# A two-layer f32r transformer trunk: inverse roots per token in the MLP, and its up tiles dealt ten and six to the two groups of down steps

## The chip, the cores and the metric

One core of one Trainium2 chip. The metric is the device time of one execution in microseconds (us); where several runs were made, their median. Engines: PE multiplies, DVE (VectorE), ACT (ScalarE) and POOL (GpSimd) work on elements, SP issues the loads.

## The reference

The trunk has two layers on 256 tokens of width D = 2048. Each adds an attention part, which the change leaves alone, and then an MLP with FF = 8192 hidden features:

```python
def rms_norm(x, g):
    y = x * rsqrt(mean(x * x, axis=-1, keepdims=True) + EPS)
    return y * g

def sq_relu_mlp(h, g, w_in, w_out):          # w_in 2048 x 8192, w_out 8192 x 2048
    return square(relu(rms_norm(h, g) @ w_in)) @ w_out

for layer in range(2):
    ...
    h = h + sq_relu_mlp(h, norm_mlp[layer], w_mlp_in[layer], w_mlp_out[layer])
```

## The kernel before

**Number format.** All products are of fp32 values. Each factor is split into two parts of the type fp32r, hi (a cast) and lo (what the cast left), and the kernel adds hi·hi, hi·lo and lo·hi. The tokens stay on chip in this form (mlpx and hid: hi in one half, lo in the other). The weights come from memory as "raw" tiles of 128x1024, 512 KB each, issued on SP into six buffers. ACT casts hi (L197; L251 and L273 for the down weights), DVE subtracts lo (L200, L252, L274). Three tiles are prepared ahead of the matmuls that use them; hi has four buffers, lo five.

**Order.** PE runs in the order in which the program is written. On DVE, ACT, POOL and SP a scheduler of the framework orders the instructions at build time, by a simulated time of its own. The calls later(…, n) and start_side(…) put small pieces of work behind a given number of the main steps' slots.

**The MLP.** The hidden features come in four chunks of sixteen tiles of 128. An up tile U multiplies two raw tiles: 16 matmuls of 512 columns with hi (they give hi·hi and the product of the tokens' lo in one go) and 16 of 256 columns with lo, all into one PSUM bank. Then ACT copies the bank's upper half (L475, low), DVE adds the lower (L1186, up), DVE takes relu and multiplies by the inverse root of the norm (L1168), ACT squares, and the square is split for the down matmuls (L1126, L1127). Because the inverse root is applied here, an up tile needs it only when it is finished, not when it is multiplied.

The output of a chunk is added up in two groups (n = 0 and 1) of 1024 columns each, but for the last chunk, whose second half is done by features or by tokens in another way. In a group, the first five pairs of hidden tiles go through a step S of Strassen's kind (seven, seven products for eight): four prepared weight pieces, 21 matmuls of 512 columns; DVE forms differences of the raw weights in place (L246 to L250), and of each pair of hidden tiles the block sums s23 and s14 (L1149 to L1152). The other three pairs go through two direct steps each, A and B, one for each 512 of the columns: 12 matmuls with one raw tile. At a group's end its banks are added to sums on chip (L1094; copies L1092 in the first chunk). In the last chunk merged (L1039) adds six sums of products to these, and turned (L1023) transposes them back and adds them to h.

**PSUM.** Of the eight banks, four ("acc") serve the up tiles and the group's sums 11, 21 and 12; two serve p1, p5 and 22; one each p6 and p7. Of the four, a group holds three from its first S on. p1, p5 and 22 share two, so that B and A steps stand where 22 has a bank.

**Turns.** A chunk's first group runs with the last eight up tiles of the same chunk, the second with the first eight of the next one. weave writes out the order. The first chunk's eight up tiles ahead of any down step are H (two tiles in halves) and T (pairs, each with two banks). In the program of before this gives, for each chunk:

```
H T2 T4 T6                                              (once)
U8 S0 U9 S1 U10 S2 U11 S3 U12 S4 U13 A5 U14 A6 U15 B5 B6 A7 B7      first group
U0 S0 A5 U1 S1 A6 U2 S2 A7 U3 S3 U4 S4 U5 U6 B5 U7 B6 B7            second group, U of the next chunk
```

A finished pair of up tiles, 2j and 2j+1, is what S_j, or A_j and B_j, of the chunk multiplies.

**The inverse root.** inverse_root sums the squares of h over the features by one fp32 matmul with a matrix of -1, whose result stands alike in all 128 partitions; DVE scales it (L576), and POOL raises 128x256 values to the power of -0.5 (L577).

Of the kernel before, what the change touches and what calls it, by code (L numbers as in the profile page):

```python
# [16 lines left out]
P = 128  # L17
D = 2048
T = 256
# [23 lines left out]
WARM_UP = 10  # L43


SEVEN = [5, 5]
BY_TURNS = 8


def weave(sevens, late):  # L50

    first, second = [], []
    u = BY_TURNS if late else 0
    for j in range(sevens):
        first += [("U", u), ("S", j)]
        u += 1
    direct = list(range(sevens, KT // 2))
    last = u + BY_TURNS - sevens
    if late:
        a, b = list(direct), list(direct)  # L60
        for i, f in enumerate(range(u, last)):
            second.append(("U", f))
            while a and 2 * a[0] + 1 < f:
                second.append(("A", a.pop(0)))
        second += [("B", j) for j in b[:-1]] + [("A", j) for j in a] + [("B", b[-1])]
    else:
        steps, first = first, []
        a = list(direct)
        for step in steps:
            first.append(step)  # L70
            if step[0] == "S" and a:
                first.append(("A", a.pop(0)))
        b = [("A", j) for j in a] + [("B", j) for j in direct]
        for f in range(u, last):
            second += [("U", f)] + ([b.pop(0)] if f > u else [])
        second += b
    return first + second


def mlp_steps(l):  # L80

    steps = [("H", 0, None)] + [("T", 0, f) for f in range(FIRST_UP, BY_TURNS, 2)]
    steps = [(c, 0) + (kind, f) for kind, c, f in steps]
    for c in range(NCH):
        for n in range(2 if c < NCH - 1 else 1):
            for kind, i in weave(SEVEN[l], n == 0):
                steps.append((c + 1 if kind == "U" and n == 1 else c, n, kind, i))
    return steps

# [40 lines left out]
def trunk(  # L130
# [161 lines left out]
    def start_side(g):  # L292
        active.append(g)
# [19 lines left out]
    def mm(o, lhs, rhs, start, stop):  # L313
        nc.tensor.matmul(o, lhs, rhs, start=start, stop=stop)
# [255 lines left out]

    def inverse_root(acc, name):

        ps = ps_y.tile([P, 512], F32, name="inv", tag="y")
        mm(ps[:, :T], neg_ones[:], acc[:], True, True)
        ri = const.tile([P, T], F32, name=f"ri_{name}", tag="ri")
        nc.vector.tensor_scalar(ri[:], ps[:, :T], -1.0 / D, EPS, op0=ALU.mult, op1=ALU.add)  # L576
        nc.gpsimd.tensor_tensor(  # L577
            ri[:], ri[:], neg_half[:, 0:1].to_broadcast([P, T]), op=ALU.pow
        )
        return ri  # L580

    def normed_heads(banks, eps_ms, gain, dst, wait=2):

# [245 lines left out]
    def mlp_stream(l):  # L829
        def unit(c, g, j):  # L830
            ap = w_down[l, 4 * g : 4 * g + 4, 2 * c + j // 4]
            ap = ap[:, :, 256 * (j % 4) : 256 * (j % 4) + 256]
            return ap.rearrange("o p x -> p o x")

        for c, n, kind, i in mlp_steps(l):
# [41 lines left out]
    def delayed(g, n):  # L877
        for _ in range(n):
            yield
        yield from g  # L880
# [57 lines left out]
    later(scale_gains, 10)  # L938

    mstat = {}  # L940
    xg = None
    xs = None

# [50 lines left out]
            two_tiles(y, [lambda b, i=i: evac(i, b) for i in (o, o + 1)], WO_ORDER)  # L994

    def mlp(l, xg_, sq, h, done):
        inv = {}
        later(lambda: inv.update(ri=inverse_root(sq, f"mlp{l}")), 4)
        sums = [heads4(f"d{l}_{i}") for i in range(4)]

        def summed(m, g):
# [45 lines left out]
                count[0] += 1  # L1047

        hid = new_act(f"hid{l}")
        sevens = SEVEN[l]  # L1050

        class Group:

# [75 lines left out]
        def block_sums(c, j, a, b):  # L1129
# [7 lines left out]
            if not whole:  # L1137
                x = nar.tile([P, T], F32R, name="s_x", tag="bias", bufs=6)
                last = (x[:, :P], x[:, P:], s14[:, P:])
            elif j != 3:  # L1140
                x = wide.tile([P, 512], F32R, name="s_x", tag="wide")
                last = (x[:, :T], x[:, T:], s14[:])
            else:
                x = [nar.tile([P, T], F32R, name="s_x", tag="bias", bufs=6) for _ in range(2)]
                last = (x[0][:], x[1][:], s14[:])
# [19 lines left out]
        def finish(c, f):  # L1165
            squares, factors = chunks[c]
            a = squares[f]
            nc.vector.scalar_tensor_tensor(  # L1168
                out=a[:], in0=a[:], scalar=0.0, in1=inv["ri"][:], op0=ALU.max, op1=ALU.mult
            )  # L1170
# [20 lines left out]

        staged = [] if l == 1 else None

        def add_second(c):
            yield from merged(1)

        def merge_first(staged=staged):
            if l == 1:
                yield from turned(3, None)
# [7 lines left out]
            yield from turned(1, done)  # L1207

        groups = {}
        for c, n, kind, i in mlp_steps(l):  # L1210
            if kind == "H":
                halves_first(xg_, FIRST_UP, lambda f, b: up(0, f, b))
                continue
            if kind == "T":
                two_tiles(xg_, [lambda b, f=f: up(0, f, b) for f in (i, i + 1)])
                continue
            if kind == "U":
                features_major(xg_, lambda b, c=c, i=i: up(c, i, b))
                continue
            if (c, n) not in groups:  # L1220
                if (c, n) == (NCH - 1, 0):
                    start_side(add_second(c))
                groups[c, n] = Group(c, n, chunks[c][1], staged if c == NCH - 1 else None)
            if kind == "S":
                groups[c, n].seven(i)
            else:
                groups[c, n].direct(i, "AB".index(kind) + 1)
# [217 lines left out]
```

## Time and profile before

| | |
|---|---|
| three runs | median 2225.76 us (2225.44 to 2228.23) |
| the profiled execution | 2227.32 us, its span 2225.6 us |
| busy share of the span | PE 97%, DVE 78%, ACT 56%, POOL 13% |
| mean granted TensorE clock | 0.992 |
| read from memory | 410.58 MB, 185 GB/s over the span |

The span is what the profiler records between the first and the last instruction. A busy share is a share of that span for one engine. In the rows of the trace "x16" is a run of that many like instructions, and brackets hold the idle time ahead of a row and the instruction that ended it. A row of the windows gives, for each stretch, its length and then the busy time (and number) of PE, PE's weight loads, DVE, ACT and POOL, the granted clock, the busy share of the DMA engines and GB/s.

### The profile page before, as it was taken

Reading aid. Unit: us, or ns where it says so; the run is one execution under the profiler, and the core shown is the slowest. Engines: PE = TensorE matmul, PEld = TensorE weight load, DVE = VectorE, ACT = ScalarE, POOL = GpSimd, SP = SyncE. Lnnn points to the kernel's source line nnn. Section 1 sums busy time; section 2 is a strip of 40 time slices with the busy share of each in tenths; the row PEclk is TensorE's granted clock in tenths of the full one; section 3 lists DMA queues with packets and bytes.
Section 4 is the critical chain, followed back from the end, with each engine's and each line's share of the span. In section 5 each row is a group of like instructions: output and inputs, shape, how many; then the busy total and the mean of one; then the engine's idle time right before and its main releaser. Section 6 shows DMA issues by size and latency. Waiting matters only on the chain.

```text
span 2225.6 us, 30260 instructions
## 1 busy us (share of the span) xinstructions
PE 2168.3 (97%) x11026; PEld 1842.7 (83%) x11026; DVE 1745.2 (78%) x2597; ACT 1246.7 (56%) x1828; POOL 285.5 (13%) x223
## 2 busy tenths in 40 slices
PE   9999999989999999999999999998899999999999
PEld 7888888877888888887888888887788888888887
DVE  7778886668789799899885556565879889889985
ACT  7645545446566566565555447554556655556563
POOL 0010103570000000000050112358000000000000
PEclk9999999999999999999999999999899999999999
DMA  9655556645665665666766563465466566666674
GB/s 329 190 161 190 176 176 198 191 141 156 207 209 168 197 211 175 194 201 179 213 179 190 182 197 116 149 193 167 133 199 208 173 197 200 189 199 183 195 212 129
DMA packets 213316, 414.64 MB, mean 186 GB/s; under 512 B 13232, under 2 KB 144304, under 8 KB 213168
## 3 DMA queue, kind: packets, MB, share of 16 engines
q1 hardware_dynamic: 212592, 410.63, 60.7%
q8 instruction: 86, 1.41, 0.3%
q10 hardware_dynamic: 576, 2.10, 0.3%
q14 instruction: 62, 0.51, 0.1%
HBM read 410.58 MB, written 2.10 MB: 185 GB/s over the span
## 4 chain that ended last, share of the span: by engine, by line
PE 87%; DVE 6%; POOL 4%; ACT 1%; issue 1%; DMA 0%; SPq 0%; ACTq 0%; DVEq 0%
PE acc L101 83%; POOL ri_mlp L577 4%; DVE lo L252 2%; PE yp L101 1%; PE accs L101 1%; PE tp L101 1%; PE s L101 1%; PE z L101 1%; ACT hi L251 0%; DVE raw L250 0%; DVE up L1168 0%; ACT hi L197 0%; DVE raw L249 0%; DVE up L1186 0%; DVE hid L1127 0%
## 5 line engine op out<-in xcount | busy, mean ns | idle before, releaser
L200 DVE TENSOR_TENSOR lo<-raw,hi 128x1024 fp32r<-128x1024 f32 (+1 forms) x524 | 640.3, 1236 | 243.1 <-ACT hi L197 211.1
L197 ACT CAST hi<-raw 128x1024 fp32r<-128x1024 f32 (+1 forms) x524 | 540.9, 1044 | 357.4 <-PE acc L101 293.1
L101 PE MATMUL acc<-mlpx,hi 128*128 128x512 f32 x2048 | 490.5, 393 | 8.9 <-DVE up L1186 8.9
L101 PE MATMUL acc<-hi,hid 128*128 128x512 f32 x1404 | 476.3, 392 | 20.1 <-ACT hid L1126 20.1
L101 PEld LDWEIGHTS acc<-mlpx,hi 128*128 128x128 f32 x2048 | 386.9, 190 | 92.1 <-issue 9.7
L251 ACT CAST hi<-raw 128x1024 fp32r<-128x1024 f32 (+1 forms) x280 | 263.8, 944 | 221.1 <-DVE raw L247 147.6
L252 DVE TENSOR_TENSOR lo<-raw,hi 128x1024 fp32r<-128x1024 f32 (+1 forms) x280 | 302.3, 1086 | 41.1 <-ACT hi L251 36.4
L101 PEld LDWEIGHTS acc<-hi,hid 128*128 128x128 f32 x1404 | 265.0, 189 | 73.3 <-ACT hid L1126 20.6
L101 PE MATMUL acc<-lo,hid 128*128 128x512 f32 x702 | 276.5, 394 | 7.9 <-DVE lo L252 7.9
L101 PEld LDWEIGHTS acc<-mlpx,lo 128*128 128x128 f32 x2048 | 261.1, 191 | 9.5 <-DVE lo L200 0.3
L101 PE MATMUL acc<-mlpx,lo 128*128 128x256 f32 x2048 | 265.0, 283 | 0.0
L101 PE MATMUL acc<-hi,xg 128*128 128x512 f32 x640 | 208.4, 398 | 0.0
L274 DVE TENSOR_TENSOR lo<-raw,hi 128x1024 fp32r<-128x1024 f32 x108 | 133.2, 1233 | 46.6 <-ACT hi L273 46.5
L101 PEld LDWEIGHTS acc<-lo,hid 128*128 128x128 f32 x702 | 132.8, 189 | 35.6 <-DVE lo L252 12.1
L273 ACT CAST hi<-raw 128x1024 fp32r<-128x1024 f32 x108 | 113.9, 1054 | 84.7 <-PE acc L101 65.6
L101 PEld LDWEIGHTS acc<-hi,xg 128*128 128x128 f32 x640 | 120.2, 188 | 24.6
L475 ACT COPY low<-acc 128x256 f32<-128x256 f32 x188 | 69.5, 369 | 111.5 <-PE acc L101 109.2
L101 PE MATMUL acc<-lo,xg 128*128 128x512 f32 x320 | 124.7, 390 | 0.7 <-DVE lo L200 0.7
L101 PE MATMUL acc<-y,hi 128*128 128x512 f32 x512 | 119.9, 391 | 0.0
L101 PEld LDWEIGHTS acc<-y,hi 128*128 128x128 f32 x512 | 95.0, 188 | 19.1
L101 PE MATMUL acc<-hi,s_w 128*128 128x512 f32 x280 | 99.5, 393 | 1.5 <-ACT hi L251 1.5
L1235 POOL TENSOR_TENSOR h<-h,dn 128x256 f32<-128x256 f32 x3 | 2.2, 733 | 660.8 <-DVE dn L1234 660.8
(207 smaller groups left out, 2739.4 us busy)
## 6 DMA issues: line engine op xcount, KB each, us to landing
raw<-in_w_up SPq DMA_DIRECT2D x256, 512.0 KB, 4.6
raw<-in_w_down SPq DMA_DIRECT2D x256, 512.0 KB, 5.7
raw<-in_w_in SPq DMA_DIRECT2D x80, 512.0 KB, 3.9
raw<-in_w_o SPq DMA_DIRECT2D x64, 512.0 KB, 4.1
raw<-in_w_mem SPq DMA_DIRECT2D x28, 512.0 KB, 6.0
raw<-in_w_kv_v SPq DMA_DIRECT2D x24, 512.0 KB, 4.2
raw<-in_w_kv_k SPq DMA_DIRECT2D x24, 512.0 KB, 4.3
raw<-in_w_q SPq DMA_DIRECT2D x24, 512.0 KB, 4.1
```

The source lines that it names most:

```text
L101: return self._tc.keep_in_program_order(fn(*args, **kwargs))
L197: nc.scalar.copy(hi[:, :n], raw[:, :n])
L200: nc.vector.tensor_tensor(lo, raw, hi.bitcast(F32), op=ALU.subtract)
L251: nc.scalar.copy(hi4, src)
L252: nc.vector.tensor_tensor(lo4, src, hi4.bitcast(F32), op=ALU.subtract)
L273: nc.scalar.copy(hi4, turned)
L274: nc.vector.tensor_tensor(lo4, turned, hi4.bitcast(F32), op=ALU.subtract)
L475: nc.scalar.copy(low[:], bank[:, T:])
L577: nc.gpsimd.tensor_tensor(ri[:], ri[:], neg_half[:, 0:1].to_broadcast([P, T]), op=ALU.pow)
L1235: nc.gpsimd.tensor_tensor(h(o), h(o), t[:], op=ALU.add)
```

## The change

Five parts, all in the MLP.

1. **inverse_root** forms the sum of squares per token: two fp32 matmuls of two columns each put it into a bank with the tokens on the partitions (stat), DVE scales 128x4 values, POOL raises these. Two slots later DVE multiplies the identity by the root (dg, twice), two fp32 matmuls with the matrix of -1 spread it over the partitions, and DVE copies it with its sign turned into ri.
2. **The turns** are a table, the same for both layers; ten up tiles stand ahead of the first down step, the first group has six and the second ten.
3. **Wide first**: each U starts with the wide matmuls (`width["last"] = "wide"`). Before, the order was the reverse of the matmuls ahead of it.
4. **Late sums**: merged(1) is started at the last chunk's first B step, not at its first S.
5. **s_x**: in the last chunk the third pair's block sums (j = 2) take two buffers of the narrow pool, not one of the wide.

```diff
-SEVEN = [5, 5]
-BY_TURNS = 8
-def weave(sevens, late):
...
+SEVEN = 5
+ALONE = 10
+TURNS = (
+    "U10 S0 U11 S1 U12 A5 S2 U13 S3 A6 U14 S4 U15 B5 B6 A7 B7",
+    "U0 S0 A5 U1 S1 A6 U2 S2 A7 U3 U4 S3 U5 U6 S4 U7 B5 U8 B6 U9 B7",
+)
+def mlp_steps():
+    steps = [(0, 0, "H", 0)] + [(0, 0, "T", f) for f in range(FIRST_UP, ALONE, 2)]
     for c in range(NCH):
         for n in range(2 if c < NCH - 1 else 1):
-            for kind, i in weave(SEVEN[l], n == 0):
+            for step in TURNS[n].split():
+                kind, i = step[0], int(step[1:])
                 steps.append((c + 1 if kind == "U" and n == 1 else c, n, kind, i))
...
     def inverse_root(acc, name):
+        ps = ps_y.tile([P, 512], F32, name="stat", tag="y")
+        for m in range(2):
+            mm(ps[:, 2 * m : 2 * m + 2], acc[:, m * P : (m + 1) * P], neg_ones[:, 0:2], True, True)
+        ms = tiny.tile([P, 4], F32, name="ms", tag="t4", bufs=8)
+        nc.vector.tensor_scalar(ms[:], ps[:, 0:4], -1.0 / D, EPS, op0=ALU.mult, op1=ALU.add)
+        r = tiny.tile([P, 4], F32, name="root", tag="t4", bufs=8)
+        nc.gpsimd.tensor_tensor(r[:], ms[:], neg_half[:], op=ALU.pow)
+        yield
+        yield
         ps = ps_y.tile([P, 512], F32, name="inv", tag="y")
-        mm(ps[:, :T], neg_ones[:], acc[:], True, True)
+        for m in range(2):
+            dg = nar.tile([P, P], F32, name="dg", tag="nar")
+            nc.vector.tensor_scalar_mul(dg[:], ident[:], r[:, 2 * m : 2 * m + 1])
+            mm(ps[:, m * P : (m + 1) * P], neg_ones[:], dg[:], True, True)
         ri = const.tile([P, T], F32, name=f"ri_{name}", tag="ri")
-        nc.vector.tensor_scalar(ri[:], ps[:, :T], -1.0 / D, EPS, op0=ALU.mult, op1=ALU.add)
-        nc.gpsimd.tensor_tensor(
-            ri[:], ri[:], neg_half[:, 0:1].to_broadcast([P, T]), op=ALU.pow
-        )
-        return ri
+        nc.vector.tensor_scalar_mul(ri[:], ps[:, :T], -1.0)
+        inverses[name] = ri
...
-        later(lambda: inv.update(ri=inverse_root(sq, f"mlp{l}")), 4)
+        start_side(delayed(inverse_root(sq, f"mlp{l}"), 4))
...
-            elif j != 3:
+            elif j < 2:
...
             if kind == "U":
+                width["last"] = "wide"
                 features_major(xg_, lambda b, c=c, i=i: up(c, i, b))
                 continue
             if (c, n) not in groups:
-                if (c, n) == (NCH - 1, 0):
-                    start_side(add_second(c))
                 groups[c, n] = Group(c, n, chunks[c][1], staged if c == NCH - 1 else None)
+            if (c, kind) == (NCH - 1, "B") and i == sevens:
+                start_side(merged(1))
```

The lines move by this: in the kernel after, the add behind an up tile is L1169 (L1186 before), its finish L1151 (L1168), the block sums L1132 to L1135 (L1149 to L1152), the split's subtraction L1110 (L1127), the group's adds L1077 (L1094), merged L1022 (L1039), the weights' lo L174 (L200) and, in an S, L226 (L252), PE's line L75 (L101).

**Where the order moves.** Three places; in the rows, a number behind a name counts the program's tiles.

DVE at the start of the first MLP, before: ri is scaled between the lo of the tile pairs T.

```order
L200 TENSOR_TENSOR lo151_4257<-raw151_4255,hi151_4256 128x1024
L1186 TENSOR_TENSOR up_4251<-acc_4178,low_4249 128x256
L576 TENSOR_SCALAR ri_mlp0_4279<-inv_4277 128x256
L200 TENSOR_TENSOR lo152_4308<-raw152_4306,hi152_4307 128x1024
L200 TENSOR_TENSOR lo153_4322<-raw153_4320,hi153_4321 128x1024
L1186 TENSOR_TENSOR up_4328<-acc_4253,low_4326 128x256
L200 TENSOR_TENSOR lo154_4340<-raw154_4338,hi154_4339 128x1024
L200 TENSOR_TENSOR lo155_4354<-raw155_4352,hi155_4353 128x1024
L1186 TENSOR_TENSOR up_4360<-acc_4254,low_4358 128x256
```

After:

```order
L1169 TENSOR_TENSOR up_4251<-acc_4178,low_4249 128x256
L551 TENSOR_SCALAR ms_4280<-stat_4277 128x4
L174 TENSOR_TENSOR lo152_4310<-raw152_4308,hi152_4309 128x1024
L559 TENSOR_SCALAR dg_4333<-ident_109,root_4282 128x128
L559 TENSOR_SCALAR dg_4336<-ident_109,root_4282 128x128
L174 TENSOR_TENSOR lo153_4324<-raw153_4322,hi153_4323 128x1024
L1169 TENSOR_TENSOR up_4330<-acc_4253,low_4328 128x256
L562 TENSOR_SCALAR ri_mlp0_4339<-inv_4332 128x256
L1151 SCALAR_TENSOR_TENSOR up_4225<-up_4225,ri_mlp0_4339 128x256
```

The scaling now gives 128x4 values, the two dg stand behind one more lo, and ri is ready ahead of the third pair; finishing (L1151) follows at once.

PE in the second group of the first chunk, before: up tile U3 with its two raw tiles, and the first matmuls of S3.

```order
L101 MATMUL acc_5517<-lo222_5734,hid0_4160 128x512
L101 MATMUL acc_5517<-hi222_5733,hid0_4160 128x512
L101 MATMUL acc_5785<-mlpx0_3213,hi223_5742 128x512 x8
L101 MATMUL acc_5785<-mlpx0_3213,hi224_5754 128x512 x8
L101 MATMUL acc_5785<-mlpx0_3213,lo223_5743 128x256 x8
L101 MATMUL acc_5785<-mlpx0_3213,lo224_5755 128x256 x8
L101 MATMUL acc_5475<-hi225_5769,hid0_4160 128x512
L101 MATMUL acc_5475<-lo225_5770,hid0_4160 128x512
```

After, U4 stands between U3 and S3; acc_5794 and acc_5855 are their banks' tiles, acc_5486 the group's sum that S3 starts with:

```order
L75 MATMUL acc_5794<-mlpx0_3213,hi223_5753 128x512 x8
L75 MATMUL acc_5794<-mlpx0_3213,hi224_5765 128x512 x8
L75 MATMUL acc_5794<-mlpx0_3213,lo223_5754 128x256 x8
L75 MATMUL acc_5794<-mlpx0_3213,lo224_5766 128x256 x8
L75 MATMUL acc_5855<-mlpx0_3213,hi225_5777 128x512 x8
L75 MATMUL acc_5855<-mlpx0_3213,hi226_5796 128x512 x8
L75 MATMUL acc_5855<-mlpx0_3213,lo225_5778 128x256 x8
L75 MATMUL acc_5855<-mlpx0_3213,lo226_5797 128x256 x8
L75 MATMUL acc_5486<-hi227_5860,hid0_4160 128x512
L75 MATMUL acc_5486<-lo227_5861,hid0_4160 128x512
```

The second up tile needs a bank of the four while 11, 21 and 12 are held: it is the one that the first up tile has.

DVE at the same place, before: lo223 and lo224 belong to U3, lo225 and what follows to S3, lo228 is S3's last.

```order
L200 TENSOR_TENSOR lo223_5743<-raw223_5741,hi223_5742 128x1024
L200 TENSOR_TENSOR lo224_5755<-raw224_5753,hi224_5754 128x1024
L252 TENSOR_TENSOR lo225_5770<-raw225_0_5765,hi225_5769 128x1024
L252 TENSOR_TENSOR lo226_5787<-raw225_1_5767,hi226_5786 128x512
L246 TENSOR_TENSOR raw225_1_5767<-raw225_1_5767 128x4x128
L247 TENSOR_TENSOR raw225_1_5767<-raw225_1_5767,raw225_0_5765 128x4x128
L249 TENSOR_TENSOR raw225_0_5765<-raw225_1_5767,raw225_0_5765 128x4x128
L250 TENSOR_TENSOR raw225_0_5765<-raw225_0_5765 128x4x128
L252 TENSOR_TENSOR lo227_5845<-raw225_1_5767,hi227_5844 128x1024
L252 TENSOR_TENSOR lo228_5851<-raw225_0_5765,hi228_5850 128x1024
L1186 TENSOR_TENSOR up_5824<-acc_5785,low_5822 128x256
```

After, lo223 to lo226 belong to U3 and U4, lo227 and lo228 are S3's first two splits, and the add out of U3's bank is up_5835:

```order
L174 TENSOR_TENSOR lo223_5754<-raw223_5752,hi223_5753 128x1024
L174 TENSOR_TENSOR lo224_5766<-raw224_5764,hi224_5765 128x1024
L174 TENSOR_TENSOR lo225_5778<-raw225_5776,hi225_5777 128x1024
L174 TENSOR_TENSOR lo226_5797<-raw226_5795,hi226_5796 128x1024
L226 TENSOR_TENSOR lo227_5861<-raw227_0_5856,hi227_5860 128x1024
L226 TENSOR_TENSOR lo228_5865<-raw227_1_5858,hi228_5864 128x512
L220 TENSOR_TENSOR raw227_1_5858<-raw227_1_5858 128x4x128
L1169 TENSOR_TENSOR up_5835<-acc_5794,low_5833 128x256
L1132 TENSOR_TENSOR s23_5841<-up_5721 128x128
L221 TENSOR_TENSOR raw227_1_5858<-raw227_1_5858,raw227_0_5856 128x4x128
L1151 SCALAR_TENSOR_TENSOR up_5835<-up_5835,ri_mlp0_4339 128x256
```

Before, the add behind U3 (L1186, up_5824) stood behind all of S3's four splits; now (L1169, up_5835) it stands behind the first two.

DVE at the first S of the last chunk, before: lo414 and lo415 are its first two splits, and the adds of merged (L1039) stand among them.

```order
L252 TENSOR_TENSOR lo414_9442<-raw414_0_9437,hi414_9441 128x1024
L1094 TENSOR_TENSOR d0_1_4154<-acc_8705,d0_1_4154 128x512
L1127 TENSOR_TENSOR s_w_9400<-s23_9398,s_w_9400 128x256
L1127 TENSOR_TENSOR s_x_9402<-s14_9399,s_x_9401 128x256
L1094 TENSOR_TENSOR d0_3_4156<-acc_9344,d0_3_4156 128x512
L1039 TENSOR_TENSOR d0_1_4154<-d0_1_4154,e0_0_4157 128x512
L252 TENSOR_TENSOR lo415_9461<-raw414_1_9439,hi415_9460 128x512
L1039 TENSOR_TENSOR d0_1_4154<-d0_1_4154,e0_1_4158 128x512
L1039 TENSOR_TENSOR e0_0_4157<-e0_0_4157,e0_2_4159 128x512
L246 TENSOR_TENSOR raw414_1_9439<-raw414_1_9439 128x4x128
```

After, with lo418 and lo419 as the first two splits and L1022 for merged:

```order
L1022 TENSOR_TENSOR d0_1_4154<-d0_1_4154,e0_0_4157 128x512
L1134 TENSOR_TENSOR s23_9547<-s14_9548,up_9472 128x128
L1110 TENSOR_TENSOR hid0_4160<-up_9541,hid0_4160 128x256
L1077 TENSOR_TENSOR d0_3_4156<-acc_9424,d0_3_4156 128x512
L1022 TENSOR_TENSOR d0_1_4154<-d0_1_4154,e0_1_4158 128x512
L1022 TENSOR_TENSOR e0_0_4157<-e0_0_4157,e0_2_4159 128x512
L1135 TENSOR_TENSOR s14_9548<-up_9541,s23_9547 128x128
L226 TENSOR_TENSOR lo419_9592<-raw418_1_9570,hi419_9591 128x512
L1110 TENSOR_TENSOR s_w_9549<-s23_9547,s_w_9549 128x256
L1022 TENSOR_TENSOR d0_3_4156<-d0_3_4156,e0_0_4157 128x512
L1110 TENSOR_TENSOR s_x_9551<-s14_9548,s_x_9550 128x256
L220 TENSOR_TENSOR raw418_1_9570<-raw418_1_9570 128x4x128
```

The adds of merged stand at the same first S in both; in the text of the program they have moved to the first B step.

More of the change, by code (lines that the diff above doesn't have):

```diff
@@ L43 @@
 WARM_UP = 10
-SEVEN = [5, 5]
-BY_TURNS = 8
-def weave(sevens, late):
[L52 to L83, printed above, removed]
+SEVEN = 5
[6 more added lines that the diff above has]
+    steps = [(0, 0, "H", 0)] + [(0, 0, "T", f) for f in range(FIRST_UP, ALONE, 2)]
     for c in range(NCH):
         for n in range(2 if c < NCH - 1 else 1):
-            for kind, i in weave(SEVEN[l], n == 0):
+            for step in TURNS[n].split():
+                kind, i = step[0], int(step[1:])
                 steps.append((c + 1 if kind == "U" and n == 1 else c, n, kind, i))
@@ L833, in unit @@
             return ap.rearrange("o p x -> p o x")
-        for c, n, kind, i in mlp_steps(l):
+        for c, n, kind, i in mlp_steps():
             if kind == "H":
@@ L940, in trunk @@
     mstat = {}
+    inverses = {}
     xg = None
@@ L996, in mlp @@
     def mlp(l, xg_, sq, h, done):
-        inv = {}
-        later(lambda: inv.update(ri=inverse_root(sq, f"mlp{l}")), 4)
+        start_side(delayed(inverse_root(sq, f"mlp{l}"), 4))
         sums = [heads4(f"d{l}_{i}") for i in range(4)]
@@ L1049, in mlp @@
         hid = new_act(f"hid{l}")
-        sevens = SEVEN[l]
+        sevens = SEVEN
         class Group:
@@ L1168, in finish @@
             nc.vector.scalar_tensor_tensor(
-                out=a[:], in0=a[:], scalar=0.0, in1=inv["ri"][:], op0=ALU.max, op1=ALU.mult
+                out=a[:], in0=a[:], scalar=0.0, in1=inverses[f"mlp{l}"][:], op0=ALU.max, op1=ALU.mult
             )
@@ L1192, in mlp @@
         staged = [] if l == 1 else None
-        def add_second(c):
-            yield from merged(1)
         def merge_first(staged=staged):
@@ L1209, in mlp @@
         groups = {}
-        for c, n, kind, i in mlp_steps(l):
+        for c, n, kind, i in mlp_steps():
             if kind == "H":
```

## The prediction

> **What bounds the kernel now.** I read the page first: TensorE (PE) is busy 97% of the span and carries 87% of the chain that ended last, with 4% on POOL. Then the waits of PE, which name what the missing time waits for (us in total, times, longest).
>
> ```profile
> PE 2168.3 (97%) x11026; PEld 1842.7 (83%) x11026; DVE 1745.2 (78%) x2597; ACT 1246.7 (56%) x1828; POOL 285.5 (13%) x223
> PE 87%; DVE 6%; POOL 4%; ACT 1%; issue 1%; DMA 0%; SPq 0%; ACTq 0%; DVEq 0%
> PE acc L101 <- ACT hid L1126: 20.1, 2, 10.1
> PE acc L101 <- DVE lo L252: 18.5, 24, 1.5
> PE acc L101 <- DVE up L1186: 8.9, 2, 4.9
> ```
>
> A wait is not all that it costs, so I laid windows over single steps of the program (first column the stretch, second its length, PEclk the granted clock). In order: a clean seven-product step S (21 matmuls), a clean up tile U, four direct steps in a row, three S that waited, and each MLP from its first up tile to the end of its last turn.
>
> ```profile
> 676.72:681.51 4.79, 4.79 (x24) 3.95 (x22) 4.17 (x6) 3.97 (x6) 0.00 (x0) 1.00 0.62 182
> 681.51:687.05 5.54, 5.54 (x34) 4.91 (x32) 5.40 (x8) 1.88 (x3) 0.00 (x0) 1.00 0.76 213
> 747.96:758.87 10.91, 10.91 (x51) 9.02 (x49) 6.95 (x10) 4.36 (x6) 0.00 (x0) 1.00 0.69 189
> 697.38:704.73 7.35, 5.64 (x23) 3.79 (x22) 5.97 (x9) 5.77 (x8) 0.00 (x0) 1.00 0.38 89
> 813.88:819.96 6.08, 5.17 (x24) 3.79 (x23) 6.05 (x9) 4.90 (x6) 0.00 (x0) 1.00 0.21 52
> 1024.38:1032.55 8.17, 5.64 (x24) 3.79 (x22) 7.39 (x12) 5.75 (x8) 0.00 (x0) 1.00 0.28 66
> 435.42:1108.30 672.88, 648.71 (x3291) 549.29 (x3290) 569.54 (x821) 387.21 (x558) 46.01 (x7) 0.99 0.63 188
> 1499.79:2173.40 673.61, 648.66 (x3292) 549.30 (x3291) 569.32 (x821) 389.05 (x563) 46.00 (x7) 0.99 0.62 188
> ```
>
> Such a stretch holds 64 U, 35 S and 42 direct steps: 64 x 5.54 + 35 x 4.79 + 42 x 10.91/4 = 636.8 us. The two stretches are 36.1 and 36.8 us longer. These 73 us are all the change can win; it leaves the matmuls as they are.
>
> **The inverse roots.** In the timeline at the start of the first MLP the column sums meet PE at 448.47, and POOL raises 128x256 values to -0.5 for 41 us. The eight up tiles run out first.
>
> ```profile
> 449.60 41.14 POOL L577 TENSOR_TENSOR ri_mlp<-ri_mlp,neg_half 128x256 f32<-128x256 f32 x1 [7.13 <-DVE ri_mlp L576]
> 496.06 0.80 PE L101 MATMUL acc<-hi,hid 128*128 128x512 f32 x1 [10.07 <-ACT hid L1126]
> 496.06:506.44 10.38, 6.40 (x21) 4.85 (x22) 10.31 (x29) 7.82 (x18) 0.00 (x0) 0.83 0.27 74
> 506.44 6.76 PE L101 MATMUL acc<-mlpx,hi 128*128 128x512 f32 x16 [3.98 <-DVE up L1186]
> 646.34 3.79 PE L101 MATMUL acc<-mlpx,hi 128*128 128x512 f32 x16
> ```
>
> PE waits 10.07; the S behind it takes 10.38 instead of 4.79 (it holds the 3.98 wait, for DVE clearing the backlog); the next 16 wide matmuls take 6.76 instead of 3.79. That is 10.07 + 5.59 + 2.97 = 18.6 us; the second MLP, whose second wait was 4.92, lost 19.6. The new form raises 128x4 values and spreads them over the tokens by a diagonal. The kernel has that form once already, in layer B:
>
> ```profile
> 1176.03 0.50 PE L101 MATMUL stat<-neg_ones,kvsq 128*128 128x2 f32 x4
> 1176.81 1.02 POOL L541 TENSOR_TENSOR r_b<-ms_b,neg_half 128x4 f32<-128x4 f32 x1 [8.46 <-DVE ms_b L537]
> 1178.45 0.48 DVE L551 TENSOR_SCALAR dg<-ident,r_b 128x128 f32<-128x128 f32 x2
> 1181.93 0.61 PE L101 MATMUL spread<-dg,neg_ones 128*128 128x128 f32 x4
> 452.84 1.05 ACT L197 CAST hi<-raw 128x1024 fp32r<-128x1024 f32 x1 [5.72 <-PE acc L101]
> 453.93 1.23 DVE L200 TENSOR_TENSOR lo<-raw,hi 128x1024 fp32r<-128x1024 f32 x1 [4.41 <-ACT hi L197]
> 450.80 14.70 PE L101 MATMUL acc<-mlpx,hi 128*128 128x512 f32 x64
> ```
>
> 1.02 us takes the place of 41.14, so the inverse is there about 33 us earlier, two more tiles stand ahead of the first S, and the whole start stall goes, with what followed it. Nothing else stands on POOL there, so its 40 us are worth nothing by themselves. Two prices remain. PE does 0.50 + 0.61 us of small fp32 matmuls instead of 0.6. And in the new DVE order the two dg stand behind the lo of the next tile, which waits for its hi: that lo ran at 453.93, so dg would be there at about 455.4, while PE reaches the spreading matmul 16 x 0.227 us after 450.80, at 454.4. I take a wait of 1.0 us per MLP; the bounds are 0 (layer B: dg 3 us early) and 1.5.
>
> **Ten tiles and six, and A steps between.** The S waits come from DVE's queue. Before the S of 697.38 it stood so:
>
> ```profile
> 697.98 0.42 DVE L1186 TENSOR_TENSOR up<-acc,low 128x256 f32<-128x256 f32 x1 [0.79 <-ACT low L475]
> 698.32 0.68 DVE L249 TENSOR_TENSOR raw<-raw,raw 128x512 f32<-128x512 f32 x1
> 699.26 1.22 DVE L252 TENSOR_TENSOR lo<-raw,hi 128x1024 fp32r<-128x1024 f32 x1
> 695.77 0.28 DVE L1152 TENSOR_TENSOR s<-up,s 128x128 f32<-128x128 f32 x1
> 660.00:830.00 170.00, 167.38 (x851) 141.58 (x850) 148.54 (x208) 98.48 (x136) 0.00 (x0) 1.00 0.65 190
> ```
>
> The add of the tile just finished stands ahead of the lo that PE needs 2 us into the S, and a pair's block sums too. Now the first group has no block sums but those of the last pair of the turn before, and an A step before its third S; in the second group two U stand before its last two S. Two cases from the new order: behind the end of the first U of a pair, up to the third split of the S that follows the pair, DVE has four raw differences, six operations of 128x256, four block sums and the split, 4 x 0.68 + 6 x 0.42 + 4 x 0.28 + 1.22 = 7.6 us; PE is there after the second U and nine matmuls of S, 5.54 + 2.1, and 1.24 more by the wait below, 8.9 us. At the first S of a middle chunk, from the end of the turn's last U on: 4 x 0.68 + 6 x 0.42 + 4 x 0.28 + up to two group adds and the half split, 3 x 0.68, + 1.22 = 9.6 us, against an A step, a U and nine matmuls, 2.73 + 5.54 + 2.1 = 10.4. So about 1 us to spare, more as DVE's operations overlap by a tenth. The S that waited before I take as free of waits but for one (late sums). DVE is busy 148.5 of 170 us (87%). A turn was 84.6 us of PE; now it is 95.7 and 73.4. Two U carry about 6 us of DVE work and a pair's block sums 2, so DVE has some 82 and 66 us of work in them, 86% and 90%: neither is bound by DVE. The loads go along: the ten-tile turn issues 36 on SP in 95.7 us, 32 in 84.6 before, the same density, so I cost them at nothing.
>
> The price is new. Four banks take the wide sums; the group holds three of them (11, 21, 12) from its first S to its last, and U uses the fourth. Where two U follow each other before the last S, the second waits until the first is out of the bank: a copy on ACT and an add on DVE.
>
> ```profile
> 513.04 2.08 PE L101 MATMUL acc<-mlpx,lo 128*128 128x256 f32 x16
> 514.96 0.40 PE L101 MATMUL acc<-hi,hid 128*128 128x512 f32 x1
> 515.22 0.37 ACT L475 COPY low<-acc 128x256 f32<-128x256 f32 x1 [0.92 <-PE acc L101]
> 515.62 0.43 DVE L1186 TENSOR_TENSOR up<-acc,low 128x256 f32<-128x256 f32 x1
> 505.88 0.41 DVE L1186 TENSOR_TENSOR up<-acc,low 128x256 f32<-128x256 f32 x1
> 649.97 4.00 PE L101 MATMUL acc<-mlpx,lo 128*128 128x256 f32 x32
> 1135.96 0.66 PE L101 MATMUL tp<-ident,d 128*128 128x128 f32 x4 [1.12 <-DVE h L1023]
> ```
>
> After this U PE went on at 514.96, and the bank was free at 516.05. Where PE waited for such an add (ended 506.29) it went on at 506.44, 0.15 later. So a second U would start at 516.20, 1.24 us late. Twice per second group, three groups, two layers: 12 x 1.24 = 14.9 us. Bounds: 0, as at 649.97, where two U share no bank (that pair stood behind the last S), and 3.98, the wait above. The row nearest is the transposes' wait for one DVE add out of their bank, 1.12; so I keep 1.24. Queued behind the waiting U on PE are only the next S and its successors; DVE and ACT use the time to get ahead.
>
> **Wide first.** U U alternated before (x32 narrow in one run); now each starts wide. The widths add up to the same 5.54, so nothing; hi is needed first, lo 3.6 us later, which is part of the slack above.
>
> **Late sums.** In the text merged(1) moves behind the last S. In DVE's order it does not: its six adds still stand ahead of the third split of the last chunk's first S, 6 x 0.68 = 4.1 us on top of the 9.6, so 3.3 us past PE's 10.4. That S took 8.17 instead of 4.79 before; I keep these 3.4 us per layer. The buffer of s_x for j = 2 only changes which pool waits; nothing.
>
> **Sum.** Per MLP there remain 636.8 + 1.1 (fp32) + 1.0 (dg) + 7.4 (six bank waits) + 3.4 (last chunk) + 0.6 for small waits = 650.3. Against 672.9 and 673.6 that is 45.9 us less. The profiled execution took 2227.32 (span 2225.60), so 2181.4; the median of the runs is 1.6 lower, which would give 2179.9. I forecast 2181.
>
> **Rivals.** (1) Bank waits hidden, or the sums late after all: the pairs cost nothing, 2166, or the last chunk's S loses its wait, 2174. Against it: three banks are held in the code, and the order shows the six adds. (2) The evacuating add is late, behind two lo and a subtraction of the next S that stand ahead of it in DVE's queue: 2.5 us per pair, and half of the S waits stay, 8 us: 2181 + 15 + 8 = 2204. For it: the add at 505.88 ended a PE wait of 3.98 us. (3) The short, repeated waits lower the clock:
>
> ```profile
> 488.20:498.50 10.30, 2.44 (x6) 1.92 (x7) 7.67 (x27) 5.13 (x17) 2.54 (x1) 0.52 0.21 79
> 505.30:512.20 6.90, 5.76 (x14) 4.58 (x15) 5.70 (x11) 1.76 (x3) 0.00 (x0) 0.53 0.30 85
> 1015.00:1060.00 45.00, 42.09 (x211) 34.74 (x210) 42.38 (x66) 24.78 (x37) 0.00 (x0) 1.00 0.56 160
> ```
>
> After the 10.07 us wait, and again after the 3.98, PE ran at half clock; the last chunk's waits (1.5 at the longest) left it at 1.00. Were each of the 12 waits to cost the 2.97 us of the half-clocked U, the time would be 2181 + 36 = 2217. [...] (4) Slower: the lo of S that stand ahead of the evacuating add wait for a weight load, and PE with them, since the add holds its bank. It decides when each pair's wait passes 1.24 + 45.9/12 = 5.1 us, a load landing some 4 us after the first U; with 7 us per pair the time is 2181 + 69 = 2250. Against it: the raw buffer comes free an S, an A and a U ahead, some 10 us, and loads of w_down land 5.7 us after issue.
>
> **Chances.** The forecast as it stands, 2174 to 2190: 0.62. Rival 1: 0.08; 2: 0.21; 3: 0.04; 4: 0.05. The range 2166 to 2202 leaves out rivals 3 and 4 and the ends of 1 and 2. What the runs can tell from no change is about 0.2%, 4.4 us: faster 0.94, same 0.01, slower 0.05.
>
> **What the changed profile would show.** Right: the new inverse at about 457, the first multiplication with it before 460 and not at 490.77; no PE wait for hid; clock 1.00 through both MLPs; PE waits for the up add 12 times, about 1.2 us each; PE waits for lo mostly in the first S of the last chunk, about 8 us long; MLP stretches of 650. Wrong: PE waits for up of 2 us and more, S of 6 to 7 us in the middle chunks, a clock of 0.5 behind the pairs, or a long wait at the first S for block sums that DVE has not done.

## The result, and the profile after

The changed kernel takes 2192.98 us (median of 4 runs, 2191.90 to 2194.17) against 2225.60 (4 runs, 2224.27 to 2228.23): a ratio of 0.9852, 95% interval 0.9835 to 0.9869. The direction was right. The time is 12 us above the forecast of 2181 and outside of the 2174 to 2190 that had a chance of 0.62; it is inside the range of 2166 to 2202 only because that reached up for rival 2, which did not come about. The profiled execution took 2191.9, its span 2190.2; the sum in the prediction was made for such an execution and gave 2181.4, so 10.5 us are to be explained.

First the page of the kernel after: busy times, and the chain that ended last, by engine.

```profile
PE 2156.7 (98%) x11038; PEld 1841.7 (84%) x11038; DVE 1743.2 (80%) x2603; ACT 1248.8 (57%) x1828; POOL 205.2 (9%) x223
PE 93%; DVE 4%; issue 1%; DMA 1%; ACT 1%; DVEq 0%; ACTq 0%
```

POOL has left the chain (4% before) and 80 us of its work are gone. What PE waits for in the kernel after (us in total, times, longest):

```profile
PE acc L75 <- DVE up L1169: 12.2, 12, 1.4
PE acc L75 <- DVE hid L1110: 6.7, 8, 0.9
PE acc L75 <- DVE lo L226: 4.4, 4, 1.4
PE inv L75 <- DVE dg L559: 1.8, 2, 0.9
```

The waits for hid of 10 us have gone, and those for lo have fallen from 18.5 us to 4.4. The twelve waits for up and the two for dg are those forecast. The second row is not: eight short waits for hid, of which the forecast had none. (A ninth, of 0.81 us, was ended by ACT's cast of hid and stands just ahead of one of the eight.)

The windows show it by place: each MLP from its first up tile to the end of its last turn; S3 with A6 behind it, in the first chunk and in the last; and the last chunk's first S.

```profile
435.13:1091.10 655.97, 642.63 (x3297) 548.03 (x3296) 568.38 (x824) 388.39 (x558) 5.88 (x7) 1.00 0.64 193
1482.63:2137.94 655.31, 642.30 (x3298) 548.08 (x3297) 568.50 (x824) 390.16 (x563) 5.87 (x7) 1.00 0.63 193
532.30:540.93 8.63, 7.80 (x36) 6.12 (x34) 7.35 (x9) 5.84 (x8) 0.00 (x0) 1.00 0.69 201
1054.55:1064.33 9.78, 8.07 (x36) 6.05 (x34) 7.35 (x9) 5.50 (x8) 0.00 (x0) 1.00 0.78 228
1017.35:1025.64 8.29, 5.84 (x23) 3.79 (x22) 7.51 (x12) 5.88 (x8) 0.00 (x0) 1.00 0.29 70
```

An MLP takes 656.0 and 655.3 us, where 650.3 was forecast, at a clock of 1.00. S3 and A6 together should take 4.79 + 2.73 = 7.52. They take 8.63 in seven of the eight first groups and 9.78 in one: 7 x 1.11 + 2.26 = 10.0 us, which is nearly all that is missing. An S with an A behind it takes 7.51 at the other places of this kernel. The wait in the row, 0.83 us, is not the whole loss of 1.11: PE's busy time is longer too, 7.80 in place of 7.52.

The timeline at the start of the first MLP shows the new root:

```profile
448.97 1.02 POOL L553 TENSOR_TENSOR root<-ms,neg_half 128x4 f32<-128x4 f32 x1 [6.79 <-DVE ms L551]
453.68 1.23 DVE L174 TENSOR_TENSOR lo<-raw,hi 128x1024 fp32r<-128x1024 f32 x1 [4.79 <-ACT hi L171]
454.82 0.47 DVE L559 TENSOR_SCALAR dg<-ident,root 128x128 f32<-128x128 f32 x2
455.24 0.68 PE L75 MATMUL inv<-dg,neg_ones 128*128 128x128 f32 x4 [0.88 <-DVE dg L559]
456.95 0.41 DVE L562 TENSOR_SCALAR ri_mlp<-inv 128x256 f32<-128x256 f32 x1
457.40 0.76 DVE L1151 SCALAR_TENSOR_TENSOR up<-up,ri_mlp 128x256 f32<-128x256 f32 x2
```

The root was there at 450.0, and dg waited almost 5 us for its turn behind a lo. PE waited 0.88 for it (forecast 1.0), and the inverse was ready at 457.4.

And the bank, between U3 and U4 of the first second group: what DVE and ACT do from the end of U3 on, and PE's next up tile.

```profile
612.58 0.37 ACT L449 COPY low<-acc 128x256 f32<-128x256 f32 x1 [0.75 <-PE acc L75]
612.58 0.69 DVE L220 TENSOR_TENSOR raw<-raw 128x512 f32<-128x512 f32 x1
613.19 0.41 DVE L1169 TENSOR_TENSOR up<-acc,low 128x256 f32<-128x256 f32 x1
613.66 1.67 PE L75 MATMUL acc<-mlpx,hi 128*128 128x512 f32 x6 [1.12 <-DVE up L1169]
```

The add came 0.24 behind the copy, since one raw difference stood ahead of it. Rival 2's delay is there in kind, a quarter of a microsecond where it needed 1.3 (2.5 us for the pair in place of 1.24).

### The profile page after: what moved, and what is told of

Read it like the earlier page. It is cut to its first block, busy times and chain, and to the rows that moved or that the text cites. A ratio compares the mean times of both kernels' runs of the same rounds, so it can differ in the third digit from the quotient of the medians.

```text
span 2190.2 us, 30309 instructions
## 1 busy us (share of the span) xinstructions
PE 2156.7 (98%) x11038; PEld 1841.7 (84%) x11038; DVE 1743.2 (80%) x2603; ACT 1248.8 (57%) x1828; POOL 205.2 (9%) x223
## 4 chain that ended last, share of the span: by engine, by line
PE 93%; DVE 4%; issue 1%; DMA 1%; ACT 1%; DVEq 0%; ACTq 0%
PE acc L75 88%; PE accs L75 1%; PE yp L75 1%; DVE lo L226 1%; DVE lo L174 1%; PE tp L75 1%; DMA raw<-in_w_down 1%; PE s L75 1%; PE z L75 1%; DVE lo L248 0%; DVE raw L220 0%; ACT hi L225 0%; DVE up L1169 0%; DVE d L1022 0%; PE cold L75 0%
## 5 line engine op out<-in xcount | busy, mean ns | idle before, releaser
L174 DVE TENSOR_TENSOR lo<-raw,hi 128x1024 fp32r<-128x1024 f32 (+1 forms) x524 | 639.5, 1236 | 242.2 <-ACT hi L171 211.9
L75 PE MATMUL acc<-mlpx,hi 128*128 128x512 f32 x2048 | 485.5, 390 | 12.2 <-DVE up L1169 12.2
L75 PE MATMUL acc<-hi,hid 128*128 128x512 f32 x1404 | 473.6, 391 | 7.5 <-DVE hid L1110 6.7
L75 PEld LDWEIGHTS acc<-mlpx,hi 128*128 128x128 f32 x2048 | 382.7, 188 | 93.3 <-DVE up L1169 14.6
L226 DVE TENSOR_TENSOR lo<-raw,hi 128x1024 fp32r<-128x1024 f32 (+1 forms) x280 | 302.9, 1087 | 50.5 <-ACT hi L225 38.8
L75 PEld LDWEIGHTS acc<-hi,hid 128*128 128x128 f32 x1404 | 263.4, 188 | 63.5 <-DVE hid L1110 10.1
L75 PE MATMUL acc<-lo,hid 128*128 128x512 f32 x702 | 274.4, 391 | 0.0
L75 PEld LDWEIGHTS acc<-mlpx,lo 128*128 128x128 f32 x2048 | 261.3, 191 | 9.0
L75 PE MATMUL acc<-mlpx,lo 128*128 128x256 f32 x2048 | 264.6, 283 | 0.0
L75 PE MATMUL acc<-hi,xg 128*128 128x512 f32 x640 | 208.4, 398 | 0.0
L75 PEld LDWEIGHTS acc<-lo,hid 128*128 128x128 f32 x702 | 132.2, 188 | 23.7
L75 PEld LDWEIGHTS acc<-hi,xg 128*128 128x128 f32 x640 | 120.2, 188 | 24.6
L75 PE MATMUL acc<-lo,xg 128*128 128x512 f32 x320 | 124.7, 390 | 0.7 <-DVE lo L174 0.7
L75 PE MATMUL acc<-y,hi 128*128 128x512 f32 x512 | 119.9, 391 | 0.0
L75 PEld LDWEIGHTS acc<-y,hi 128*128 128x128 f32 x512 | 95.0, 188 | 19.1
L75 PE MATMUL acc<-hi,s_w 128*128 128x512 f32 x280 | 98.1, 390 | 0.5 <-ACT hi L225 0.5
L1154 ACT ACTIVATE up<-up 128x256 f32<-128x256 f32 x128 | 52.6, 414 | 48.9 <-DVE up L1151 48.9
```

Of the source, the lines that this page charges most:

```text
L75: return self._tc.keep_in_program_order(fn(*args, **kwargs))
L174: nc.vector.tensor_tensor(lo, raw, hi.bitcast(F32), op=ALU.subtract)
L226: nc.vector.tensor_tensor(lo4, src, hi4.bitcast(F32), op=ALU.subtract)
```

## The experiments

**Which part takes the stall away?** The kernel before with the new inverse root alone, and the kernel after with the old one alone:

```diff
 # e1: before, with the new inverse_root (...) and its start
-        later(lambda: inv.update(ri=inverse_root(sq, f"mlp{l}")), 4)
+        start_side(delayed(inverse_root(sq, f"mlp{l}"), 4))
 # e2: after, with the old inverse_root (...) and its start
-        start_side(delayed(inverse_root(sq, f"mlp{l}"), 4))
+        later(lambda: inv.update(ri=inverse_root(sq, f"mlp{l}")), 4)
```

> The kernel before with the new inverse root and nothing else: the old turns, eight up tiles ahead of the first S. Theory (the root alone takes away the start stall, and the other parts of the change earn little or nothing together): the PE wait of 10.07 us before the first S, the S of 10.38 us and the half clock behind it go, 18.6 and 19.6 us, less some 1.5 us per layer for the wait for dg and the fp32 matmuls; the waits of the S steps for lo stay, 17 us per layer: 2190 us, as fast as the changed kernel (2193) or faster. Rival (both are needed: with eight tiles ahead DVE's backlog of finished tiles still holds up the first S and the second up tile): about half of the stall is left, 2207 us.

> The changed kernel with the old inverse root (POOL raises 128x256 values for 41 us); turns and the rest as changed. Theory (ten tiles ahead would by themselves cover most of the 41 us): the roots are there at about 491 us of the first MLP, PE reaches the first S at about 498, so the wait of 10 us is gone, but DVE's backlog of ten unfinished tiles still costs some 5 us per layer: 2200 to 2205 us. Rival (without the new root nothing of the start stall goes): wait of PE for hid of 5 us or more, half clock behind it, 2225 to 2230 us.

e1 took 2203.97 us (ratio to before 0.9894, 0.9881 to 0.9908). It earned 22 us against the 2225.60 above (23 in its own runs), where the theory had 35 and the rival 18: the rival is nearer. In e1 the stretch from the first S of an MLP to the next up tile, and the waits for lo, read so:

```profile
487.63:495.62 7.99, 5.29 (x24) 3.71 (x22) 7.81 (x14) 6.52 (x12) 0.00 (x0) 1.00 0.42 136
PE acc L101 <- DVE lo L252: 19.7, 26, 1.5
```

The root alone takes the 10 us wait away, but that stretch still takes 7.99 for 4.79, with DVE busy 7.81 of it: the S itself 6.05, and then 1.94 in which the next up tile waits for a bank. Eight tiles ahead leave DVE's backlog in the way. The waits for lo stay as they were (18.5 before). The other four parts of the change, taken together, earned the rest, 11 us.

e2 took 2230.64 us (1.0017, 1.0008 to 1.0026): 0.2% slower than before, at the upper end of what the rival said. My theory, that ten tiles ahead would by themselves cover most of the 41 us, fell. The timeline of e2 tells why:

```profile
449.34 41.14 POOL L551 TENSOR_TENSOR ri_mlp<-ri_mlp,neg_half 128x256 f32<-128x256 f32 x1 [7.13 <-DVE ri_mlp L550]
494.28 2.10 DVE L1143 SCALAR_TENSOR_TENSOR up<-up,ri_mlp 128x256 f32<-128x256 f32 x6
500.62 0.42 DVE L1161 TENSOR_TENSOR up<-acc,low 128x256 f32<-128x256 f32 x1
501.19 5.34 PE L75 MATMUL acc<-mlpx,hi 128*128 128x512 f32 x16 [9.91 <-DVE up L1161]
```

The root was done at 490.5. The six tiles that waited for it are finished from 494.28 on, and only behind them and their block sums comes the add that empties a bank. PE wanted that bank for the next up tile at 491.3. The same 10 us of waiting are there, now for up; the rival had them at hid. More tiles ahead cover a late value only as long as the banks last.

**The wait for hid.** U13's tile is multiplied by A6. In the kernel after, the timeline of DVE behind U13, which ends at 532.30, and PE's entry into the second half of A6:

```profile
532.91 0.43 DVE L1169 TENSOR_TENSOR up<-acc,low 128x256 f32<-128x256 f32 x1
533.86 1.23 DVE L226 TENSOR_TENSOR lo<-raw,hi 128x1024 fp32r<-128x1024 f32 x1 [0.52 <-PE acc L75]
535.00 0.42 DVE L1151 SCALAR_TENSOR_TENSOR up<-up,ri_mlp 128x256 f32<-128x256 f32 x1
535.33 1.22 DVE L248 TENSOR_TENSOR lo<-raw,hi 128x1024 fp32r<-128x1024 f32 x1
536.47 2.35 DVE L174 TENSOR_TENSOR lo<-raw,hi 128x1024 fp32r<-128x1024 f32 x2
538.74 0.42 DVE L1110 TENSOR_TENSOR hid<-up,hid 128x256 fp32r<-128x256 f32 x1
539.21 0.73 PE L75 MATMUL acc<-hi,hid 128*128 128x512 f32 x2 [0.83 <-DVE hid L1110]
```

A tile's way from its last matmul to a split hid is add, finish, square, cast, subtraction, and four lo stand between them: 6.9 us. PE is there after an S and half an A, 4.79 + 1.36 = 6.2. e3 puts an up tile more between:

```diff
-    "U10 S0 U11 S1 U12 A5 S2 U13 S3 A6 U14 S4 U15 B5 B6 A7 B7",
+    "U10 S0 U11 S1 U12 A5 S2 U13 S3 U14 A6 S4 U15 B5 B6 A7 B7",
```

> The changed kernel with A6 of the first group one step later, behind U14 (U13 S3 U14 A6 S4 in place of U13 S3 A6 U14 S4). Theory (A6 multiplies the hidden tile of U13, which is split only some 7 us after U13's last matmul, and PE comes to it after 4.8 + 1.8 us): the eight waits of PE for hid (0.81 to 0.90 us each, 9.7 us of lost time by the excess of the stretches of down matmuls over 0.229 us a matmul) go: 2183 us. Rival (DVE is behind there, whatever PE does next): S4, now without an up tile between A6 and itself, waits for its lo instead, 2190 to 2193 us.

e3 took 2183.25 us (0.9802, 0.9789 to 0.9816): 9.7 us less than the kernel after, as much as was expected from the rows (the windows above give 10.0). PE's waits in e3:

```profile
PE acc L75 <- DVE up L1169: 13.1, 12, 1.6
PE acc L75 <- DVE lo L226: 4.4, 4, 1.4
```

No wait for hid is left, and S4 does not wait in its place.

**The bank.** e4 keeps the two up tiles ahead of S3 and S4 but puts the direct step between them:

```diff
-    "U0 S0 A5 U1 S1 A6 U2 S2 A7 U3 U4 S3 U5 U6 S4 U7 B5 U8 B6 U9 B7",
+    "U0 S0 A5 U1 S1 U2 S2 U3 A6 U4 S3 U5 A7 U6 S4 U7 B5 U8 B6 U9 B7",
```

> The changed kernel with the second group as U0 S0 A5 U1 S1 U2 S2 U3 A6 U4 S3 U5 A7 U6 S4 U7 B5 U8 B6 U9 B7: a direct step of 2.73 us stands between the two up tiles of a pair, so the one bank that is left has time to come free (1.24 us). Theory (the bank alone makes the second up tile wait): all twelve PE waits for up go, 12 x 1.23 = 14.8 us, and S1 and S2, which lose the A steps ahead of them, wait at most 1 us a group: 2178 to 2184 us. Rival (the A steps ahead of S were what kept DVE in time): as much comes back as waits for lo in S1 and S2, 2.5 us each, 2190 us or more.

e4 took 2176.53 us (0.9774, 0.9761 to 0.9787), 16.5 less than the kernel after. PE's waits:

```profile
PE acc L75 <- DVE hid L1110: 6.7, 8, 0.9
PE acc L75 <- DVE lo L226: 4.4, 4, 1.4
```

All twelve waits for up are gone and the waits for lo have not grown, though S1 and S2 of the second group have lost the A steps ahead of them. So the second up tile of each pair paid 1.37 us for the bank (1.24 forecast; its wait in the rows is 1.02 on the mean), and nothing was bought with it that a direct step between does not give too.

**The small parts.** e5 takes away the wide start and the other buffer of s_x, e9 the wide start alone:

```diff
 # e5 and e9
-                width["last"] = "wide"
                 features_major(xg_, lambda b, c=c, i=i: up(c, i, b))
 # e5 only
-            elif j < 2:
+            elif j != 3:
```

> The changed kernel without two of its small parts: an up tile that follows an up tile starts narrow again, and s_x of the third pair (j = 2) takes one wide buffer again. Theory (both cost and earn nothing): within 2 us of the changed kernel, 2191 to 2195 us, the same PE waits. Rival (wide first is what gives the second up tile of a pair its lo in time): PE waits for lo at the twelve second up tiles, about 1 us each, 2200 us or more.

> The changed kernel without the wide start alone: an up tile that follows an up tile starts narrow. Theory (the 7 us that the two undone parts cost together are the width's: the second up tile keeps its hi tiles to its end, so the cast of S's first pieces, and the load behind it, come later, and the add out of the bank stands behind them in DVE's order): 2200 us, PE waits for up of 1.7 us on the mean of twelve. Rival (s_x in a wide buffer, which moves DVE's order from the second group of the first chunk on, costs it): 2193 us.

e5 took 2199.99 us (0.9881, 0.9866 to 0.9897), e9 2200.88 (0.9888, 0.9872 to 0.9905). In e5 the theory failed and the rival had the time, but not the place: PE waits no longer for lo, it waits longer for up. e9 took the 2200 us of its theory, with waits for up of 1.44 us on the mean in place of 1.7. In e9 that row, SP's issue of the two loads of S4's raw tiles, and ACT's cast of the second of them; then the same two places in the kernel after:

```profile
PE acc L75 <- DVE up L1169: 17.3, 12, 2.4
620.63 2.46 SPq L208 DMA_DIRECT2D raw<-in_w_down  x2
630.12 0.62 ACT L225 CAST hi<-raw 128x512 fp32r<-128x512 f32 x1 [2.38 <-DMA raw<-in_w_down]
```

```profile
618.38 2.05 SPq L208 DMA_DIRECT2D raw<-in_w_down  x2
627.99 0.62 ACT L225 CAST hi<-raw 128x512 fp32r<-128x512 f32 x1 [0.76 <-PE acc L75]
```

The load is issued about 2 us later and ACT waits for it. DVE's lo waits for that cast, and the add out of the bank stands behind that lo. So the wide start was worth 7.9 us here. In the profiled executions, which lie 9.4 us apart, some 5 are these waits and some 4 are two stretches at half clock. One stands behind a wait for up, where the granted clock is 0.50 from 632.35 to 635.76 and 16 narrow matmuls take 3.57 us, in place of 2.08 in the kernel after (at 617.46):

```profile
632.58 3.57 PE L75 MATMUL acc<-mlpx,lo 128*128 128x256 f32 x16 [2.21 <-DVE up L1169]
```

The other stands behind the last chunk's first S in the first MLP; the kernel after has waits there too, at a clock of 1.00 (last section). That the loads are late because a tile that starts narrow keeps its hi buffers to its end is argued from the code; the runs show the late load and its followers. This is the chain of rival 4 in small: the longest of the waits is 2.4 us, where rival 4 needed 5.1.

**Late sums.** e11 starts merged(1) at the last chunk's first S, as before; e6 holds its adds on DVE behind what the program has written for DVE up to there:

```diff
 # e6, in merged
-                nc.vector.tensor_tensor(dst, dst, src, op=ALU.add)
+                pin(nc.vector.tensor_tensor(dst, dst, src, op=ALU.add), n == 1)
```

> The changed kernel with merged(1) started at the last chunk's first S again, as before. Theory (the move in the text changed nothing, since the adds stand at the same place in DVE's order around that S): 2193 us, that S 8.3 us long. Rival (the order further down differs, and the late start earned something there): 2197 us or more.

> The changed kernel with the six adds of merged(1) held on DVE behind what the program has written for DVE up to there, so that they really come at the last chunk's first B step. Theory (they are what makes the last chunk's first S late): that S falls from 8.3 to 4.8 us in both layers, 2 x 3.5 us, 2186 us. Rival (the block sums, the group's adds and the split are too much there by themselves): it still takes 7 us or more, 2190 to 2193 us.

e11 took 2193.74 us (0.9857, 0.9841 to 0.9873), the changed kernel's time, with the same waits: as written, the move changed nothing. e6 took 2188.69 us (0.9831, 0.9817 to 0.9845), a gain of 4.3 where 7 were expected. Its windows over the last chunk's first S and over a stretch at that chunk's end, and PE's two waits just ahead of the latter:

```profile
1017.62:1022.41 4.79, 4.79 (x23) 3.95 (x22) 4.41 (x6) 4.52 (x7) 0.00 (x0) 1.00 0.46 120
1084.86:1088.28 3.42, 3.42 (x8) 2.70 (x9) 0.83 (x2) 0.14 (x1) 0.00 (x0) 0.50 0.70 187
```

```profile
1083.35 0.50 PE L75 MATMUL acc<-hi,hid 128*128 128x512 f32 x1 [1.21 <-ACT hid L1109]
1084.79 1.18 PE L75 MATMUL acc<-hi,hid 128*128 128x512 f32 x2 [0.71 <-DVE hid L1110]
```

The S takes its clean 4.79, so the six adds were its whole delay. But in the first layer the late adds now stand among the steps that finish U15, and A7, two B steps behind it, waits for its tile: 1.21 and 0.71 us, and then 3.4 us at half clock.

**All together.** e7 has the turns of e3 and of e4; e8 adds e6's pin and spreads the root one slot later (a third `yield`); e10 is e8 with the root spread as in the change, and dg made on ACT:

```diff
 # e10
-            nc.vector.tensor_scalar_mul(dg[:], ident[:], r[:, 2 * m : 2 * m + 1])
+            nc.scalar.activation(dg[:], ident[:], AF.Copy, scale=r[:, 2 * m : 2 * m + 1])
```

> The changed kernel with both turns altered: A6 of the first group behind U14, and in the second group a direct step between the up tiles of a pair. Theory (the two costs are separate): 2193.0 less 9.7 less 16.5 gives 2167 us, with no PE wait for up and none for hid. Rival (both live on the same slack of DVE): waits for lo in S3 or S4 of the first group, 2171 us or more.

> e7 with the adds of merged(1) held late as in e6, and the spreading of the inverse root one slot later. Theory: another 7 us by the sums and 1 to 2 us by the dg waits of 0.88 us, 2158 to 2160 us. Rival: the two dg, one tile later in DVE's order, are again behind a lo that waits for its hi, so only the sums count, 2160 to 2161 us; if the late adds collide with the end of the MLP, 2164 us.

> e8 with the spreading of the inverse root two slots after the root again, as in the changed kernel, and with the two dg on ACT in place of DVE. Theory (dg is late only because it stands behind a lo in DVE's order): the two PE waits for dg of 0.88 us go, 2160.2 less 1.8 gives 2158.4 us. Rival (ACT's order puts dg behind a cast that waits for its raw tile): the wait stays or grows, 2160 to 2163 us.

e7 took 2167.29 us (0.9735, 0.9721 to 0.9749): the two costs add up. e8 took 2160.17 (0.9703, 0.9690 to 0.9717), the fastest here, 65.9 us below the kernel before in its runs (2226.06). Here the late sums earn their 7 us without e6's new wait. The windows of e8's two MLPs:

```profile
435.12:1074.66 639.54, 638.66 (x3298) 547.98 (x3297) 568.00 (x823) 386.46 (x558) 5.88 (x7) 1.00 0.65 198
1466.17:2105.89 639.72, 638.84 (x3298) 547.90 (x3296) 567.09 (x822) 388.23 (x563) 5.88 (x7) 1.00 0.65 198
```

They stand 2.7 and 2.9 us above the 636.8 of their clean steps. The wait for dg did not go, neither by the later slot nor on ACT, where it doubled, as the rivals of e8 and e10 had it; first its row in e8, then ACT and PE in e10:

```profile
PE inv L75 <- DVE dg L560: 1.8, 2, 0.9
```

```profile
454.61 1.04 ACT L171 CAST hi<-raw 128x1024 fp32r<-128x1024 f32 x1 [0.76 <-PE acc L75]
455.83 0.69 ACT L559 ACTIVATE dg<-ident,root 128x128 f32<-128x128 f32 x2
456.28 0.78 PE L75 MATMUL inv<-dg,neg_ones 128*128 128x128 f32 x4 [1.71 <-ACT dg L559]
```

In both, dg stands in a queue behind a cast or a lo that waits for PE to give back a buffer. e10 took 2161.94 us (0.9714, 0.9699 to 0.9728).

## Why the prediction was right or wrong

- **The start stall.** Right in size: no wait of 10 us, no half clock behind it (1.00 over both MLPs), dg 0.88 us for 1.0. Its cause was told in half: "two more tiles stand ahead of the first S" was put as a bonus, but e1 and e2 show that both parts are needed, the early root and the later first S, and the root alone leaves 3.2 us at the first S of e1 and the up tile behind it.
- **S waits of the middle chunks.** Right: taken as free, and the four waits for lo that are left are all in the last chunk's first S (8.29 us, "about 8" forecast). The 3.4 us per layer kept for the late sums measured 3.5, and e6 and e11 bear out the reading of DVE's order. (By its rows a turn of six up tiles is 73.6 us, not 73.4; nothing hangs on it.)
- **The bank.** Right in mechanism, 14.9 us forecast; e4 gave back 16.5. Of the bounds, 0 to 3.98, the row of 1.12 was the one to follow.
- **The direct steps: the step that failed.** The prediction checked each S against its lo and each U against its bank, and gave the A steps only as time that lies between ("an A step before its third S"). It never asked when A6's own tile is ready. The order puts A6 4.79 us behind U13; the term was 0 and measured 10.0 us by the windows, 9.7 by e3. The rows to price it stood in the profile of before, where an A step had an up tile more between itself and its second tile. There U12 has an S behind it, as U13 has now; the S starts at 547.01, and U12's tile is split at 555.64:

```profile
547.01 0.40 PE L101 MATMUL acc<-hi,hid 128*128 128x512 f32 x1
555.22 0.42 DVE L1127 TENSOR_TENSOR hid<-up,hid 128x256 fp32r<-128x256 f32 x1
```

That is 8.6 us, against the 6.2 us after which PE reaches A6's second tile in the new order.

- **Wide first, costed at nothing.** Right about the widths, wrong as a statement on the part: without it the kernel is 7.9 us slower (e9). It did not enter the sum, since the sum was made for the order with it; the s_x buffer shows nothing in the times (e5 and e9 differ by 0.9 us), though a microsecond or two may hide behind their different stretches at half clock (mean clocks of the profiled executions 0.999 and 0.998).
- **Rivals.** 1 did not come about (the pairs were not hidden, the last chunk's S kept its wait). 2 is there with 0.24 us of delay where it needed 1.3. 3: in the profiled execution the clock stayed at 1.00 through both MLPs with twelve waits of about a microsecond, 17.1 us and more from one to the next (two of the other runs had mean clocks of 0.998 and 0.999, so it need not always). 4 did not come about; e9 shows its chain in small.

## What to carry to other kernels

When an order of steps is changed, list for each step every operand that was made shortly before (weights, bank, and the activations too), and compare the time its makers take through their queues with the time the consumer takes to get there. Where two producers share the last free bank, put a step that needs no bank between them; and a value that comes late is hidden by more work ahead only if that work can give back its own buffers without it. Moving a statement in the text may move nothing when a scheduler orders the engine: read the order that comes out.

## What the runs showed of the hardware

In e6 two waits of 1.21 and 0.71 us are followed by half clock (0.50 for 3.42 us). In the kernel after, longer single waits are not: the clock is 1.00 around the wait for up of 1.39 us that ended at 1661.42. It is 1.00 too in the first S of the last chunk in the first MLP, where the waits are 1.43, 0.26 and 0.77 us. e9 has the same S, the last chunk's first, once with a drop and once without. Its windows over that S and the 16 wide matmuls behind it, in the first MLP and in the second:

```profile
1022.34:1031.65 9.31, 6.99 (x23) 4.56 (x22) 8.53 (x13) 6.13 (x8) 0.00 (x0) 0.82 0.32 83
1031.65:1036.94 5.29, 5.29 (x17) 4.18 (x16) 4.94 (x7) 1.67 (x2) 0.00 (x0) 0.67 0.83 239
2074.34:2082.62 8.28, 5.81 (x24) 3.79 (x23) 7.50 (x12) 5.87 (x8) 0.00 (x0) 1.00 0.28 71
2082.62:2086.25 3.63, 3.63 (x18) 3.00 (x16) 3.56 (x5) 0.82 (x2) 0.00 (x0) 1.00 0.71 254
```

The drop cost 1.03 + 1.66 us. By these rows PE was idle for 2.32 us of the S with the drop and for 2.47 us of the S without: the sum of the waits in an S does not tell the two apart. The stretches at half clock differ in length: 3.41 us in e9 (632.35 to 635.76), 3.42 in e6, and in the kernel before 10.24 us (488.69 to 498.93) and 6.82 (505.76 to 512.58), which begin within the waits of 10.07 and 3.98 us. What decides whether short waits are followed by half clock was not shown.
